# A recurrent gate's square roots taken in one step, and its scan steps spread over other places of a projection, in a two-layer decoder trunk

## The chip, the cores and the metric

One core of a Trainium2 chip (trn2) runs the whole kernel. The metric is the device time of one execution in microseconds (us). A time is told as the median of several executions; a profile is one execution of its own, with its own time.

## The reference

A two-layer decoder trunk on 256 positions of width 2048, batch 1, in float32. The change lies in layer 0, which projects the normed input to six column groups and feeds two recurrent mixers side by side:

```python
def rg_lru(xb, w_a, b_a, w_i, b_i, lam):
    r = sigmoid(einsum(xh, w_a) + b_a)
    i = sigmoid(einsum(xh, w_i) + b_i)
    log_a = -LRU_C * r * softplus(-lam)
    a = exp(log_a)
    u = sqrt(-expm1(2.0 * log_a)) * (i * xf)
    h = associative_scan(h_t = a_t * h_(t-1) + u_t)

def recurrent_mixers(h, ...):
    x_lru, y_lru, q_h, f_h, v_h, g_h = split(h @ w_in)     # six groups of 1024 columns
    lru = rg_lru(causal_depthwise_conv(x_lru), ...) * gelu(y_lru)
    hg = hgrn2(q_h, f_h, v_h, g_h, ...)                    # a gated linear recurrence, 8 heads of 128
    return concatenate([lru, hg]) @ w_out
```

A squared-ReLU MLP follows, then layer 1 (dilated attention and a second MLP) and a last norm.

## The kernel before, in words

**Matmuls.** Every weight block of 128x2048 floats (a unit) is loaded by SP into one of three `raw` buffers, then split in two: ScalarE (ACT) rounds it into `hi` with a CAST, and VectorE (DVE) makes the remainder `lo` with a TENSOR_TENSOR (`Weights.split`, L142). TensorE (PE) multiplies activations, split the same way, with both. `unit` (L249) fetches the unit two places ahead whenever one begins.

**The order of the work in layer 0.** The input projection runs in groups of 512 columns, in the order `v0 x0 x1 q0 G0 f0 q1 f1 G1 v1 g0 y0 g1 y1` (`ORDER`); `G0` and `G1` are the gate matmuls of the two halves of the LRU (`lru_gates`, L683), which share one 8x256 buffer per half (called `bufb` in the profile, gates r in its first four columns blocks, gates i in the last four). A group is four units, and a unit here is twice 12 matmuls of 128x512 (8 with `hi`, 4 with `lo`), once for each half of the positions (`tokens`, L373). So a group has eight places, one behind each run of 12 matmuls.

**The lanes.** What the mixers do beside the projection is written as Python generators, and a table (`TICKS`, L1246) says for each group which of them takes a step at which of its eight places; `.` is no step. A generator's step ends at its `yield`; when a generator is exhausted, the next one of the lane begins in the same step. The lanes that matter here:

- `e` is `lru_scan(0)`, then `lru_scan(1)` (L696). Each has four steps. The first two take two of the four feature blocks each: on DVE the product of gate i and the input (`xc`), on ACT tanh and exp of gate r, on DVE a TENSOR_SCALAR. The last two again take two blocks each: on ACT the square root, on DVE a SCALAR_TENSOR_TENSOR, a product and the scan along the positions.
- `a` and `b` are `hgrn(0)`, `hgrn(2)` and `hgrn(1)`, `hgrn(3)` (L541), two heads each; `hgrn(2)` and `hgrn(3)` are the second half, and their steps come together at one place. Step 1 turns the queries on PE (banks `pd` and `pt`) and takes their sigmoid on ACT. Step 2 turns the gates f (banks `pl`), takes three activations and two scalings of them on ACT. Step 3 makes products on DVE (`st`), rounds them on ACT and takes remainders on DVE (`bufb`, `near`). Step 4 is the first that has PE multiply them (`pd<-bufb,ones_r`, `pl<-near,ones_r`, then the same in `pt` and `pl`); steps 5 to 10 double a block size each, step 11 copies one product (`st<-pl`), step 12 multiplies with the values (`po` in the banks `pd` and `pt`) and takes squares and a copy of the result on ACT (`ho`).

**Order on the engines.** While these lanes run, ACT and DVE are held to the order in which the program issues (`InOrder`, L58). PE has an order of its own (`chain`), which runs through the matmuls of the projection and those of the lanes alike: a lane's matmul that waits holds the projection's behind it. ACT keeps the tables of one kind of function at a time (`tables`, L287): exp and tanh, sigmoid, square root; a change of kind is an ACT_TABLE_LOAD. `lut` (L291) holds functions of one kind together.

**Banks.** A group's two sums lie in two of three `p` banks. At the end of a group, ACT copies them out (`tk<-p`, L422); the first half of the next group gets the third bank, and its second half must wait for the first of these copies.

Of the kernel before, what the change touches and what calls it, by code (L numbers as in the profile page):

```python
# [15 lines left out]
AF = mybir.ActivationFunctionType  # L16
# [25 lines left out]
def trunk_kernel(ctx, tc, head, x, xtok, xback, cols, tab, masks, pos, fin, w_in, w_gate, w_out, w_qkv, w_o, w1, w2, out):  # L42
# [238 lines left out]
    def after(ins, names):  # L281
        ins = getattr(ins, "ins", ins)
        for n in names:
            tc.add_manual_dep(ins, n, NOSYNC, reason="order on one engine")
        return ins.name
# [5 lines left out]
    def lut(out_, in_, func, **kw):  # L291
        i = A.activation(out_, in_, func, **kw)
        if luts["kind"] != tables[func]:
            luts.update(kind=tables[func], before=luts["now"], now=[])
        luts["now"].append(after(i, luts["now"][:1] or luts["before"]))
# [140 lines left out]
    m = tmp.tile([P, 2], F32, name="nm2", bufs=2)  # L436
# [259 lines left out]
    def lru_scan(gp):  # L696
        gr, gi = rooms[gp][:, :4], rooms[gp][:, 4:]
        for half in range(2):
            for m in range(2 * half, 2 * half + 2):
                b = 4 * gp + m  # L700
                V.tensor_tensor(xc[:, b], xc[:, b], gi[:, m], OP.mult)
                lut(gi[:, m], gr[:, m], AF.Tanh, scale=sp4[:, b:b + 1])
                lut(gr[:, m], gr[:, m], AF.Exp, scale=sp8[:, b:b + 1])
                V.tensor_scalar(gi[:, m], gi[:, m], -1.0, 1e-30, op0=OP.mult, op1=OP.max)
            yield
        for half in range(2):
            for m in range(2 * half, 2 * half + 2):
                b = 4 * gp + m
                lut(gi[:, m], gi[:, m], AF.Sqrt)
                V.scalar_tensor_tensor(gi[:, m], gr[:, m], 1.0, gi[:, m], op0=OP.add, op1=OP.mult)  # L710
                V.tensor_tensor(xc[:, b], xc[:, b], gi[:, m], OP.mult)
                V.tensor_tensor_scan(xc[:, b], gr[:, m], xc[:, b], 0.0, op0=OP.mult, op1=OP.add)
            yield
# [19 lines left out]
    def reload():  # L733
        for j in range(2):
# [3 lines left out]
                 c=[lru_in(0, 0), lru_in(0, 1), lru_in(1, 0), lru_in(1, 1),  # L738
                    lru_gelu(0), lru_out(0, 0), lru_out(0, 1), lru_gelu(1), lru_out(1, 0), lru_out(1, 1)],
                 e=[lru_scan(0), lru_scan(1)],  # L740
                 d=[finish(0, 0), finish(0, 1), finish(1, 0), finish(1, 1)])
    InOrder.on = True
# [442 lines left out]
    with urgent():  # L1185
        for j in range(2):
            m = tmp.tile([P, 1], F32, name="fm", bufs=2)
# [175 lines left out]
```

## Time and profile before

| what | value |
| --- | --- |
| median of 3 runs (least, most) | 2119.51 us (2119.07, 2119.61) |
| the profiled execution: its own time | 2119.95 us |
| its span, first to last instruction | 2118.20 us |
| busy in the span: PE, DVE, ACT, POOL | 2105.5, 1792.0, 1321.5, 72.3 us |
| mean granted PE clock | 0.997 of full speed |
| group v1 on PE, from its first matmul to g0's | 180.03 to 207.22 us |

Rows of the timeline give the start in us from the span's beginning, the length in us, the engine, the line, the operation, output<-inputs, and how many instructions the row joins; in brackets stands how long the engine was idle ahead of it and what ended that. L68 is the line of the helper that issues nearly everything on ACT and DVE, so rows are told apart by their tiles: `hi` and `lo` are weights, `xc` and `bufb` with 256 columns the LRU, `bufb` with 512 columns and `near`, `st`, `xall` the second mixer.

### The profile page before, as it was taken

The page shows a single profiled execution, that of the slowest core. Times are in us where ns is not written, and L with a number is a line of the kernel's source. Part 1 is how long each engine was busy: PE and PEld are TensorE (multiplying, and loading weights), DVE is VectorE, ACT ScalarE, POOL GpSimd, SP SyncE. Part 2 cuts the span into 40 slices and gives each one's busy share as a digit, 9 for nine tenths or more (in the row PEclk, how much of TensorE's full clock was granted, in tenths as well). Part 3 has the DMA queues.
Part 4 walks back from the last instruction along what each step waited for, and adds up shares of the span by engine and source line. Part 5 has one row for each costly group of instructions (what it writes and reads, how often), then busy time and mean ns, then how long its engine had stood idle before and what let it go on. Part 6 is the DMA issues. An engine that isn't in the chain of part 4 may idle for free.

```text
span 2118.2 us, 24850 instructions
## 1 busy us (share of the span) xinstructions
PE 2105.5 (99%) x9712; PEld 1752.8 (83%) x9712; DVE 1792.0 (85%) x1742; ACT 1321.5 (62%) x1356; POOL 72.3 (3%) x89
## 2 busy tenths in 40 slices
PE   9999999999999999999999999999999999999998
PEld 7888788888888888888888888888888888888887
DVE  7686878988888888889998888798988987988887
ACT  7576556675566566566665666576755755755764
POOL 0000000000000000000000000000000000000000
PEclk9999999999999999999999999999999999999999
DMA  8544456787787878877778667477778778787884
GB/s 344 181 162 159 157 208 209 248 267 236 244 262 252 258 230 274 253 242 237 263 252 255 203 214 238 179 236 236 243 244 272 242 237 276 245 250 239 277 261 157
DMA packets 70453, 500.15 MB, mean 236 GB/s; under 512 B 7872, under 2 KB 8128, under 8 KB 10560
## 3 DMA queue, kind: packets, MB, share of 16 engines
q1 hardware_dynamic: 58176, 413.29, 50.7%
q0 software_dynamic: 11872, 84.94, 22.1%
q8 instruction: 76, 1.25, 0.2%
q10 hardware_dynamic: 288, 0.34, 0.0%
q14 instruction: 41, 0.34, 0.0%
HBM read 496.44 MB, written 2.10 MB: 235 GB/s over the span
## 4 chain that ended last, share of the span: by engine, by line
PE 98%; ACT 1%; DVE 1%; DMA 0%; SPq 0%; issue 0%; DVEq 0%
PE p L261 62%; PE pd L261 15%; PE po L261 14%; PE pt L261 3%; PE pl L264 2%; PE pl L261 1%; DMA both_in<-in_head 0%; ACT xall L68 0%; ACT L68 0%; ACT hi L68 0%; PE po L264 0%; ACT ho L68 0%; DVE xall L68 0%; DVE xc L68 0%; DVE bufb L68 0%; ACT bufb L68 0%
## 5 line engine op out<-in xcount | busy, mean ns | idle before, releaser
L68 ACT CAST hi<-raw 128x2048 fp32r<-128x2048 f32 (+1 forms) x364 | 660.1, 1819 | 518.5 <-PE p L261 300.7
L68 DVE TENSOR_TENSOR lo<-raw,hi 128x2048 fp32r<-128x2048 f32 (+1 forms) x364 | 788.9, 2172 | 137.2 <-ACT hi L68 136.6
L261 PE MATMUL p<-hi,bufa 128*128 128x512 f32 x2000 | 504.2, 393 | 0.7 <-ACT hi L68 0.6
L261 PEld LDWEIGHTS p<-hi,bufa 128*128 128x128 f32 x2000 | 373.2, 189 | 76.8 <-ACT hi L68 1.3
L261 PE MATMUL p<-hi,bufb 128*128 128x512 f32 x1264 | 318.3, 391 | 0.0
L68 DVE TENSOR_TENSOR lo<-s,hi 128x2048 fp32r<-128x2048 f32 x120 | 274.3, 2286 | 12.9 <-ACT hi L68 10.9
L261 PEld LDWEIGHTS p<-hi,bufb 128*128 128x128 f32 x1264 | 236.3, 188 | 48.5 <-DVE bufb L68 0.2
L261 PE MATMUL p<-lo,bufa 128*128 128x512 f32 x1000 | 270.2, 390 | 0.0
L68 ACT CAST hi<-s 128x2048 fp32r<-128x2048 f32 x120 | 229.4, 1911 | 58.2 <-PE pd L261 23.6
L261 PEld LDWEIGHTS p<-lo,bufa 128*128 128x128 f32 x1000 | 188.1, 188 | 40.0 <-DVE lo L68 0.7
L261 PE MATMUL p<-lo,bufb 128*128 128x512 f32 x632 | 173.0, 390 | 0.0
L261 PEld LDWEIGHTS p<-lo,bufb 128*128 128x128 f32 x632 | 118.7, 188 | 24.7
L68 DVE TENSOR_TENSOR lo<-t,hi 128x2048 fp32r<-128x2048 f32 x40 | 91.5, 2287 | 4.4 <-ACT hi L68 4.0
L68 ACT CAST hi<-t 128x2048 fp32r<-128x2048 f32 x40 | 76.6, 1915 | 28.2 <-PE pd L261 12.3
L68 DVE TENSOR_TENSOR s<-s,raw 128x2048 f32<-128x2048 f32 x40 | 91.3, 2284 | 1.1 <-DMA raw<-in_w_qkv 1.1
L68 DVE TENSOR_TENSOR s<-raw,t 128x2048 f32<-128x2048 f32 x40 | 91.4, 2286 | 0.3 <-DMA raw<-in_w_o 0.2
L68 ACT ACTIVATE y<-y 128x512 f32<-128x512 f32 x112 | 70.5, 629 | 31.8 <-DVE y L68 31.0
L261 PE MATMUL pd<-hi,bufa 128*128 128x512 f32 x352 | 88.2, 393 | 0.0
L261 PE MATMUL p<-hi,formx 128*128 128x512 f32 x352 | 87.7, 391 | 0.0
L68 DVE SCALAR_TENSOR_TENSOR xall<-p,nm,xall 128x512 f32<-128x512 f32 x64 | 47.9, 748 | 43.3 <-PE p L261 43.3
L261 PE MATMUL po<-hi,bufb 128*128 128x512 f32 (+1 forms) x320 | 78.2, 386 | 0.0
L261 PEld LDWEIGHTS p<-hi,formx 128*128 128x128 f32 x352 | 65.7, 188 | 13.4
(309 smaller groups left out, 2573.1 us busy)
## 6 DMA issues: line engine op xcount, KB each, us to landing
raw<-in_w SPq DMA_DIRECT2D x224, 1024.0 KB, 6.9
raw<-in_w_in SPq DMA_DIRECT2D x45, 1024.0 KB, 4.8
raw<-in_w_qkv SPq DMA_DIRECT2D x42, 1024.0 KB, 7.2
t<-in_w SPq DMA_DIRECT2D x32, 1024.0 KB, 7.2
t<-in_w POOLq DMA_DIRECT2D x32, 1024.0 KB, 9.0
s<-in_w POOLq DMA_DIRECT2D x32, 1024.0 KB, 9.2
raw<-in_w_out SPq DMA_DIRECT2D x15, 1024.0 KB, 4.8
raw<-in_w_o SPq DMA_DIRECT2D x15, 1024.0 KB, 4.8
```

The lines of the kernel that those rows point to most:

```text
L68: i = call(*args, **kw)
L261: chain[:] = [after(T.matmul(*args, **kw), chain)]
L264: chain[:] = [after(T.transpose(out_, in_, ident), chain)]
```

## The change

```diff
@@ lru_scan
             yield
+        for m in range(4):
+            lut(gi[:, m], gi[:, m], AF.Sqrt)
         for half in range(2):
             for m in range(2 * half, 2 * half + 2):
                 b = 4 * gp + m
-                lut(gi[:, m], gi[:, m], AF.Sqrt)
                 V.scalar_tensor_tensor(gi[:, m], gr[:, m], 1.0, gi[:, m], op0=OP.add, op1=OP.mult)
@@ TICKS
-    "v1": "ab . ab e ab e ab e",
-    "g0": "ab e ab . ab . ab .",
+    "v1": "ab e ab e ab e ab e",
+    "g0": "ab . ab . ab . ab .",
```

Two things. In both halves of the LRU, the third step now takes all four square roots, and the fourth takes none. And `lru_scan(1)` has its four steps at the places 1, 3, 5 and 7 of v1 (counted from 0), where it had them at 3, 5 and 7 of v1 and 1 of g0. The first half keeps its places in f0. PE's order of instructions is the same in both kernels.

**ACT, at the place 1 of v1** (`sp4` and `sp8` are the scales of tanh and exp, `st<-pl` is step 11 of the second mixer's first half, `c__91` the gate biases; the difference of the two kernels):

```order
 L68 ACTIVATE bufb_1497<-pl,c__91 128x256 x2
-L68 CAST hi<-raw 128x2048 x2
+L68 CAST hi<-raw 128x2048
+L68 ACTIVATE bufb_1497<-bufb_1497,sp_364 128x256
+L68 ACT_TABLE_LOAD
+L68 ACTIVATE bufb_1497<-bufb_1497,sp_362 128x256
+L68 ACTIVATE bufb_1497<-bufb_1497,sp_364 128x256
+L68 ACTIVATE bufb_1497<-bufb_1497,sp_362 128x256
+L68 CAST hi<-raw 128x2048
 L68 COPY st<-pl 128x2x128 x2
```

The first scan step, with its table load, now stands ahead of the CAST of v1's last unit and of the two copies of step 11, and not behind them.

**ACT, from the place 6 of v1 on, before** (`pd` and `pt` hold the queries of step 1, `tk<-p` are the copies at the end of v1; behind the last row follow step 2's activations, one more load and the roots of the other two blocks):

```order
L68 COPY ho_1688<-pt_1681 128x512
L68 ACTIVATE bufb3_1497<-bufb3_1497,sp4_364 128x256
L68 ACTIVATE bufb3_1497<-bufb3_1497,sp8_362 128x256
L68 ACTIVATE bufb3_1497<-bufb3_1497,sp4_364 128x256
L68 ACTIVATE bufb3_1497<-bufb3_1497,sp8_362 128x256
L68 CAST hi_1717<-raw_1715 128x2048
L68 ACT_TABLE_LOAD
L68 ACTIVATE xall_79<-pd_1732 128x2x2x128
L68 ACTIVATE xall_79<-pt_1740 128x2x2x128
L68 ACT_TABLE_LOAD
L68 ACTIVATE bufb3_1497<-bufb3_1497 128x256 x2
L68 ACTIVATE tk_1769<-p_1558,nr2_317 128x512
```

and now:

```order
L68 COPY ho_1696<-pt_1689 128x512
L68 ACT_TABLE_LOAD
L68 ACTIVATE bufb3_1497<-bufb3_1497 128x256 x4
L68 CAST hi_1727<-raw_1725 128x2048
L68 ACT_TABLE_LOAD
L68 ACTIVATE xall_79<-pd_1742 128x2x2x128
L68 ACTIVATE xall_79<-pt_1750 128x2x2x128
L68 ACTIVATE tk_1777<-p_1558,nr2_317 128x512
L68 ACTIVATE tk_1777<-p_1559,nr2_317 128x512
L68 CAST hi_1784<-raw_1782 128x2048
```

The four roots stand together behind step 12's copies and ahead of a unit's CAST; the sigmoid of step 1, step 2 and, later, the output gate's sigmoid share one table load. From v1's beginning to that sigmoid there were six table loads and are three.

**DVE, ahead of step 3** (`st<-xall` is step 3's first product, before):

```order
L68 TENSOR_TENSOR lo_1777<-raw_1774,hi_1776 128x2048
L68 SCALAR_TENSOR_TENSOR bufb3_1497<-bufb3_1497 128x256
L68 TENSOR_TENSOR xc_403<-xc_403,bufb3_1497 128x256
L68 SCALAR_TENSOR_TENSOR xc_403<-bufb3_1497,xc_403 128x256
L68 SCALAR_TENSOR_TENSOR bufb3_1497<-bufb3_1497 128x256
L68 TENSOR_TENSOR xc_403<-xc_403,bufb3_1497 128x256
L68 SCALAR_TENSOR_TENSOR xc_403<-bufb3_1497,xc_403 128x256
L68 TENSOR_TENSOR st_1851<-xall_79 128x2x256
```

and now:

```order
L68 SCALAR_TENSOR_TENSOR bufb3_1497<-bufb3_1497 128x256
L68 TENSOR_TENSOR xc_403<-xc_403,bufb3_1497 128x256
L68 SCALAR_TENSOR_TENSOR xc_403<-bufb3_1497,xc_403 128x256
L68 SCALAR_TENSOR_TENSOR bufb3_1497<-bufb3_1497 128x256
L68 TENSOR_TENSOR xc_403<-xc_403,bufb3_1497 128x256
L68 SCALAR_TENSOR_TENSOR xc_403<-bufb3_1497,xc_403 128x256
L68 TENSOR_TENSOR lo_1785<-raw_1782,hi_1784 128x2048
L68 TENSOR_TENSOR st_1851<-xall_79 128x2x256
```

The last two scans (the SCALAR_TENSOR_TENSOR that writes `xc`) changed places with the remainder of a unit of g0, and their roots are no longer taken just ahead of them.

## The prediction

> **What bounds the kernel now.** I read the page's first part, then PE's waits, then PE's timeline around each wait.
>
> ```profile
> PE 2105.5 (99%) x9712; PEld 1752.8 (83%) x9712; DVE 1792.0 (85%) x1742; ACT 1321.5 (62%) x1356; POOL 72.3 (3%) x89
> PE pd L261 <- ACT bufb L68: 1.5, 1, 1.5
> PE pt L261 <- ACT bufb L68: 0.9, 1, 0.9
> PE pd L261 <- DVE bufb L68: 0.6, 1, 0.6
> PE pt L261 <- DVE bufb L68: 0.3, 1, 0.3
> ```
>
> PE bounds the kernel: it is busy for 2105.5 us of a span of 2118.2. So an edit on ACT and DVE is worth only what it takes from PE's waits, and four of the few waits there are (3.3 us together) stand at one place, where step 4 of the second half's `hgrn` waits for step 3's products. The timeline of PE at this place, in g0:
>
> ```profile
> 220.81 1.07 PE L261 MATMUL p<-lo,bufa 128*128 128x512 f32 x4
> ...
> 223.35 0.50 PE L261 MATMUL pd<-bufb,ones_r 128*128 128x512 f32 x1 [1.48 <-ACT bufb L68]
> ...
> 227.21 0.79 PE L261 MATMUL pt<-bufb,ones_r 128*128 128x512 f32 x1 [0.34 <-DVE bufb L68]
> ...
> 228.23 3.62 PE L261 MATMUL p<-hi,bufa 128*128 128x512 f32 x8
> ...
> 235.74 1.07 PE L261 MATMUL pl<-xall,kc 128*128 128x128 f32 x8
> ```
>
> and at the same step of the first half, in q1, where nothing waits:
>
> ```profile
> 137.48 1.07 PE L261 MATMUL p<-lo,bufa 128*128 128x512 f32 x4
> 138.39 0.61 PE L261 MATMUL pd<-bufb,ones_r 128*128 128x512 f32 x2
> ...
> 139.77 1.99 PE L261 MATMUL p<-hi,bufa 128*128 128x512 f32 x8
> ...
> 145.22 1.07 PE L261 MATMUL pl<-xall,kc 128*128 128x128 f32 x8
> ```
>
> The instructions are the same. Undisturbed, step 4 begins 0.91 us after the `lo` row, takes 1.38 (138.39 to 139.77), and step 5 follows 5.45 later (145.22). In g0, step 4 could begin at 220.81 + 0.91 = 221.72, and step 5 at 221.72 + 6.83 = 228.55. It begins at 235.74. So the place costs **7.19 us**, more than twice the idle time that is listed: the rest is the clock.
>
> ```profile
> 222.30:225.70 3.40, 1.24 (x4) 0.67 (x4) 3.30 (x7) 1.32 (x3) 0.00 (x0) 1.00 0.00 0
> 225.80:232.50 6.70, 6.08 (x15) 4.51 (x15) 6.67 (x12) 2.95 (x5) 0.00 (x0) 0.50 0.26 83
> ```
>
> (The stretch, its length, then the busy time of PE and of the others.) The granted clock, third figure from the end, is 0.50 from 225.8 to 232.5, 6.7 us long, behind 3.4 us in which PE was busy for 1.24. That is why eight matmuls at 228.23 take 3.62 us, and eight at 139.77 take 1.99.
>
> What holds step 3 up is DVE:
>
> ```profile
> 210.10 0.42 DVE L68 SCALAR_TENSOR_TENSOR bufb<-bufb 128x256 f32<-128x256 f32 x1
> ...
> 213.13 2.27 DVE L68 TENSOR_TENSOR lo<-raw,hi 128x2048 fp32r<-128x2048 f32 x1
> 218.95 0.42 DVE L68 SCALAR_TENSOR_TENSOR bufb<-bufb 128x256 f32<-128x256 f32 x1 [3.56 <-ACT bufb L68]
> ...
> 221.98 0.67 DVE L68 TENSOR_TENSOR st<-xall 128x512 f32<-128x512 f32 x1
> ...
> 227.08 0.42 DVE L68 TENSOR_TENSOR near<-st,near 128x256 fp32r<-128x256 f32 x1
> 218.50 0.72 ACT L68 ACTIVATE bufb<-bufb 128x256 f32<-128x256 f32 x2
> ```
>
> DVE waits 3.56 us for the second pair of roots (ACT, 218.50), scans two blocks in 3.03 us (218.95 to 221.98), and only then begins step 3, which ends at 227.50 with `near`; PE takes up the projection at 228.23, 0.7 us behind.
>
> **The change part by part.** In the new order DVE still does two scans ahead of step 3, but waits for no root there. When it gets there is a chain through ACT and DVE from v1 on; it starts at a row that the change leaves where it is:
>
> ```profile
> 185.57 4.49 DVE L68 TENSOR_TENSOR lo<-raw,hi 128x2048 fp32r<-128x2048 f32 x2
> 189.98 0.42 DVE L68 TENSOR_TENSOR xc<-xc,bufb 128x256 f32<-128x256 f32 x1
> 207.91 2.28 DVE L68 TENSOR_TENSOR lo<-raw,hi 128x2048 fp32r<-128x2048 f32 x1
> 190.49 0.51 ACT L68 ACTIVATE bufb<-bufb,sp 128x256 f32<-128x256 f32 x1
> ...
> 193.68 1.89 ACT L68 CAST hi<-raw 128x2048 fp32r<-128x2048 f32 x1
> 197.01 0.28 ACT L68 ACTIVATE ho<-pd 128x128 f32<-128x128 f32 x1 [1.44 <-PE pd L261]
> ...
> 200.32 1.05 ACT L68 ACTIVATE bufb<-bufb,sp 128x256 f32<-128x256 f32 x2
> ...
> 202.49 1.90 ACT L68 CAST hi<-raw 128x2048 fp32r<-128x2048 f32 x1
> 204.41 1.28 ACT L68 ACT_TABLE_LOAD   x1
> 205.70 0.60 ACT L68 ACTIVATE xall<-pd 128x512 f32<-128x512 f32 x1
> ...
> 208.73 1.25 ACT L68 ACTIVATE tk<-p,nr 128x512 f32<-128x512 f32 x2
> 206.33 0.88 DVE L68 SCALAR_TENSOR_TENSOR xall<-pd,omlb,xall 128x256 f32<-128x256 f32 x2 [3.96 <-ACT xall L68]
> ```
>
> 1. One remainder, not two, stands ahead of the first `xc` product. A remainder takes 2.19 us from start to start (207.91 to the scan row 210.10), so the product starts at 185.57 + 2.19 = 187.76, and the first scan step ends with ACT's CAST at 193.68 - 2.22 = 191.46, done at 193.35.
> 2. That CAST's remainder takes DVE from 193.4 to 195.6; then comes the second step's product, and 0.51 later (189.98 to 190.49) its tanh, at 196.1. The two pairs take 2.17 (200.32 to 202.49), so the CAST of g0's first unit runs from 198.3 to 200.2.
> 3. Step 12's squares and copies take 3.31 (197.01 to 200.32): to 203.5. Then the new load, 1.28, to about 204.9; four roots for 1.4 (two took 0.72); a CAST of 1.9, to 208.1; the load of the sigmoid, to 209.4; the sigmoid of 0.60, to 210.0.
> 4. DVE has scanned the first two blocks by then (3.03 from 205.3). Its four products of step 1 take 1.58 (206.33 to 207.91): 211.6. A remainder, 2.19: 213.8. The two other scans, 3.03: 216.8. A remainder, 2.19: **219.0**, where step 3 begins, instead of 221.98.
>
> So step 3 and all that follows on DVE shifts by **3.0 us**. Its input is there: step 2's activations end on ACT at about 217, as before, since the copies ahead of them come some 1.6 us later and a load and a pair of roots less stand between. Step 3 ends at 227.50 - 3.0 = 224.5, and PE takes up the projection at about 224.6. Nominally it would be 221.72 + 1.38 = 223.1, so some 1.5 us of the wait remain. With the clock whole, step 5 follows 5.45 us later, at 230.1, against 235.74: **5.6 us are saved**. Of these, 3.6 are in the restart (228.23 to 224.6) and 2.1 in matmuls that are no longer slow (7.51 from restart to step 5 before, 5.45 now).
>
> The rest, each costed at nothing or nearly:
> - Three table loads of 1.28 us less on ACT. ACT is busy 62% of the span, and only those on the chain above count.
> - The second half of g0's first unit waits for the first `tk<-p`. It follows item 3's sigmoid and its twin (0.5 each), so it runs from 210.4 to about 211.1. PE wants the bank here:
>
> ```profile
> 210.74 2.07 PE L261 MATMUL p<-hi,bufa 128*128 128x512 f32 x8
> 195.47 1.50 PE L261 MATMUL pd<-tk,st 128*128 128x128 f32 x12
> raw<-in_w_in SPq DMA_DIRECT2D x45, 1024.0 KB, 4.8
> ```
>
>   That is a new wait of 0.3 us, but it ends ahead of step 4, where PE waits for DVE in any case; so it adds nothing to the sum.
> - Step 11's copies now stand behind the moved CAST, at 193.3 to 194.1; PE wants them at 195.47. Cover 1.4 us; beyond that each us costs one.
> - SP's queue: the buffer of v1's last unit comes free at 195.6 and not at 190.06, and the next load into it lands 4.8 us later, 200.4. Its CAST stands at 211.4 in the new order. POOL has no work here.
> - The first half's roots: one CAST moves back by two roots, 0.6 us. Its remainder starts behind a scan in both kernels:
>
> ```profile
> 116.46 1.90 ACT L68 CAST hi<-raw 128x2048 fp32r<-128x2048 f32 x1
> 119.78 2.27 DVE L68 TENSOR_TENSOR lo<-raw,hi 128x2048 fp32r<-128x2048 f32 x1
> ```
>
>   The CAST would end at 119.0, ahead of 119.78, so nothing moves.
> - After step 5, PE is the bound again, and ACT and DVE run earlier too, DVE by only 3.0 us at first. So up to 0.2 us may be lost at step 5, where the copies `kc` come close; I count none.
>
> The profiled execution took 2119.95 us, 0.44 above the median, so the sum goes on the median: 2119.51 - 5.6 = **2113.9 us**.
>
> Two rules were weighed. ACT's row of a table load is 1.28 us, its neighbours lie 0.02 us from it (202.49 + 1.90 to 204.41, and to 205.70), and the chain above holds three loads. The Trainium skill, page "ScalarE: Activation LUTs", section "What ACT_TABLE_LOAD costs", gives about 1.28 us and a drain of 1.38 us on top for every change. By that, as an estimate from that page, step 3 would begin some 4 us later and the gain would be 1.5 us; the trace here has no room for such a drain, so it gets no chance of its own. In the other rule the skill speaks for the change: in the page "TensorE: Matmul & The Clock Gate", section "What's actually happening", the clock falls only after about 3.4 us of idleness. By this rule it would stay whole in the new kernel; but here it fell with no wait over 1.48 us, so the trace does not bear that limit out.
>
> **The rivals.**
> *The clock falls all the same.* The remaining 1.5 us of waiting lies in some 3 us of step 4. If that is enough, the half clock lasts about as long as before, 6.7 us, and costs up to 3.4 us: gain 2.2, **2117.3 us**. For it: the clock fell with matmuls between the waits. Against it: there PE was busy for 1.24 of 3.4 us; here, with 1.5 us of waits in such a stretch, it would be for 1.9, somewhat over half. And early in the trace half a microsecond of idleness leaves the clock whole:
>
> ```profile
> 5.00:6.00 1.00, 0.50 (x2) 0.37 (x3) 0.96 (x3) 0.60 (x2) 0.00 (x0) 1.00 1.01 372
> ```
>
> *The wait goes entirely*, because the chain runs 1.5 us earlier than I add up: gain 7.2, **2112.3 us**.
> *Slower: the bank.* The `tk` copy stands behind four roots and two loads, and holds PE at 210.74. I have it 0.3 us late. If ACT's chain runs late by x, this wait and step 3 both come late by x, and PE loses it whole. The gain is gone from x = 5.6 on, and with a second fall of the clock (3.4 us) from x = 2.2 on; an x of 6.5 with it gives 2119.5 + 4.3 = **2123.8 us**. Against it: each term is a measured row, and between 194.1 and 196.1 ACT is idle.
> *The change does nothing that shows*: another instruction at DVE's head holds step 3 as long as now, **2119.5 us**. The order shows none.
>
> **How the numbers follow.** The forecast has 0.64, the wait that goes entirely 0.05, the falling clock 0.18, nothing 0.06, slower 0.07. About 0.2%, 4.2 us, is what a measurement of this kernel can tell from no change. The forecast's 5.6 lies 1.4 above that, and its chain may be off by about 1, so I put 0.04 of it below: faster 0.65, same 0.28, slower 0.07. The range goes from the whole wait gone (2112.2) to the falling clock (2117.6), which holds 0.85.
>
> **What the new profile would show.** Right: `st<-xall` on DVE near 219.0, PE back in the projection near 224.6, `pl<-xall,kc` near 230.1, the clock at 1.00 from 224 to 234, two waits of PE left at step 4 (near 0.4 and 0.9 us) and one of 0.3 ahead of 210.74's row. Wrong: a clock of 0.50 anywhere in g0; a wait at 195.47; or a time after 250 that isn't shifted by the same 5.6 us, which would mean that loads or DVE take the gain back later.

## The result, and the profile after

The changed kernel takes 2114.26 us (median of 12 executions, 2113.83 to 2114.61), the kernel before beside it 2119.34 us (12 executions, 2118.21 to 2120.23): ratio 0.9976, with a 95% interval from 0.9967 to 0.9985. The profiled execution took 2114.33 us and spans 2112.6, against 2119.95 and 2118.2.

The busy times of the page and the waits of PE, of the changed kernel:

```profile
PE 2103.1 (100%) x9712; PEld 1751.9 (83%) x9712; DVE 1791.8 (85%) x1742; ACT 1317.2 (62%) x1353; POOL 72.3 (3%) x89
PE pt L261 <- DVE bufb L68: 0.6, 1, 0.6
PE pt L261 <- ACT bufb L68: 0.2, 1, 0.2
```

Of the four waits at step 4, two of 0.6 and 0.2 us are left. PE's busy time fell by 2.4 us though it has the same 9712 instructions. Most of that is the clock: from PE's return to the projection to step 5 it took 7.51 us before and takes 5.47 now (224.50 to 229.97). The timeline of PE in g0:

```profile
208.84 1.07 PE L261 MATMUL p<-lo,bufa 128*128 128x512 f32 x4
...
210.71 2.12 PE L261 MATMUL p<-hi,bufa 128*128 128x512 f32 x8
...
221.73 0.62 PE L261 MATMUL pd<-bufb,ones_r 128*128 128x512 f32 x2
...
222.79 0.51 PE L261 MATMUL pt<-bufb,ones_r 128*128 128x512 f32 x1 [0.21 <-ACT bufb L68]
223.93 0.50 PE L261 MATMUL pt<-bufb,ones_r 128*128 128x512 f32 x1 [0.63 <-DVE bufb L68]
...
224.50 2.00 PE L261 MATMUL p<-hi,bufa 128*128 128x512 f32 x8
...
229.97 1.23 PE L261 MATMUL pl<-xall,kc 128*128 128x128 f32 x8
```

and the windows of the same stretches as before (length, busy time of PE, PEld, DVE, ACT, POOL, then the granted clock):

```profile
222.30:225.70 3.40, 2.55 (x13) 1.77 (x12) 3.37 (x5) 2.66 (x3) 0.00 (x0) 1.00 0.15 60
225.80:232.50 6.70, 6.70 (x35) 5.62 (x34) 6.70 (x12) 2.84 (x5) 0.00 (x0) 1.00 0.46 159
```

Step 4 takes 2.77 us (221.73 to 224.50) where 1.38 is undisturbed, so 1.4 us of its wait remain. The clock stays at 1.00, no wait stands ahead of step 12's matmuls (the forecast had named one there as a sign of being wrong), and the whole span is 5.6 us shorter, so nothing later takes the gain back. For all runs below I use one distance, **the place**: from the first `lo` row of g0 to step 5's first `pl<-xall,kc`. It doesn't depend on where a whole profile begins; the rows of PE ahead of 180 us differ by up to 0.7 us between two profiles. In the kernel before the first `lo` row is this:

```profile
209.03 1.07 PE L261 MATMUL p<-lo,bufa 128*128 128x512 f32 x4
```

So the place was 235.74 - 209.03 = 26.71 us before. It is 229.97 - 208.84 = 21.13 now, 5.58 less, and undisturbed it would be 19.52 (12.69 from 209.03 to 221.72, and the 6.83 of the prediction).

### The profile page after: what moved, and what is told of

Same layout as the page of the kernel before. It is cut to its first block, busy times and chain, and to the rows that moved or that the text cites. A ratio compares the mean times of both kernels' runs of the same rounds, so it can differ in the third digit from the quotient of the medians.

```text
span 2112.6 us, 24846 instructions
## 1 busy us (share of the span) xinstructions
PE 2103.1 (100%) x9712; PEld 1751.9 (83%) x9712; DVE 1791.8 (85%) x1742; ACT 1317.2 (62%) x1353; POOL 72.3 (3%) x89
## 4 chain that ended last, share of the span: by engine, by line
PE 98%; DVE 1%; ACT 1%; issue 0%; DVEq 0%; ACTq 0%
PE p L261 62%; PE pd L261 15%; PE po L261 14%; PE pt L261 3%; PE pl L264 2%; PE pl L261 1%; DVE lo L68 0%; ACT hi L68 0%; DVE xall L68 0%; PE po L326 0%; ACT L68 0%; ACT bufb L68 0%; PE po L264 0%; ACT ho L68 0%; DVE st L68 0%
```

## The experiments

Eleven runs, on three chips; the kernel before ran on each of these chips too (2119.34, 2119.26 and 2118.96 us). Differences below are to the kernel before on the same chip.

### The grouped roots alone

The new generator with the old table.

```diff
-    "v1": "ab e ab e ab e ab e",
-    "g0": "ab . ab . ab . ab .",
+    "v1": "ab . ab e ab e ab e",
+    "g0": "ab e ab . ab . ab .",
```

> The four roots in one step, the steps at the places of before. Theory (the time follows the moment at which DVE begins step 3, and the clock): with the roots of all four blocks taken at the place 7 of v1, DVE's last two scans in g0 no longer wait 3.56 us for ACT. On DVE the remainder at 213.1 ends at 215.3, the scans take 3.0, step 3 starts near 218.4 instead of 222.0, PE is back in the projection near 224.0 instead of 228.2, the clock stays whole: 6.1 us less than before, about 1 us less than the whole change, so the moved places are worth nothing or a little less than nothing. Rival A (the places do it: a free place 1 in g0): same as before. Rival B (each table load less is worth the same, three loads for 5.1 us; here two are gone): 3.4 us less.

Measured: 2113.92 us (8 executions), ratio 0.9975 [0.9965, 0.9985], 5.4 us less than before. On PE and on DVE:

```profile
208.38 1.07 PE L261 MATMUL p<-lo,bufa 128*128 128x512 f32 x4
...
229.03 1.23 PE L261 MATMUL pl<-xall,kc 128*128 128x128 f32 x8
```

```profile
212.48 2.27 DVE L68 TENSOR_TENSOR lo<-raw,hi 128x2048 fp32r<-128x2048 f32 x1
214.66 0.42 DVE L68 SCALAR_TENSOR_TENSOR bufb<-bufb 128x256 f32<-128x256 f32 x1
...
217.69 0.67 DVE L68 TENSOR_TENSOR st<-xall 128x512 f32<-128x512 f32 x1
```

The 3.56 us for which DVE waited for a root are gone (214.66 follows its remainder at once), though the last scan step still stands in g0. The place is 20.65, 6.06 less than before and 0.48 less than in the whole change: step 3 begins 9.31 us behind the first `lo` row, in the whole change 9.77. So the roots edit alone does all that the change does. The expected 6.1 us is what the place shows; the medians show 5.4, and the lead over the whole change at the place is half of the expected 1 us.

### The places alone

The old generator with the new table (the two lines above with their signs exchanged, in the kernel before).

> The steps at the new places, each step with its own two roots, as before. Theory: ACT has the load and the second pair of roots ahead of the copy that frees the bank, and another load ahead of step 2, so step 2 ends near 219.8 and a CAST stands between it and step 3's rounding; the copy comes 1.4 us late for PE, step 3's last row ends near 226.1 on DVE, PE is back near 226.2 instead of 228.2: 1.8 us less than before if the clock falls again, 3.9 us less if it does not. Rival A (the places do it): 5 us less. Rival B (one load is gone): 1.7 us less, with step 3 at any time.

Measured: 2116.14 us (11 executions), 0.9985 [0.9976, 0.9994], 3.2 us less. PE's timeline and two windows:

```profile
208.54 1.07 PE L261 MATMUL p<-lo,bufa 128*128 128x512 f32 x4
...
211.83 2.11 PE L261 MATMUL p<-hi,bufa 128*128 128x512 f32 x8 [1.34 <-ACT tk L68]
...
231.44 1.23 PE L261 MATMUL pl<-xall,kc 128*128 128x128 f32 x8
```

```profile
209.41:212.83 3.42, 2.08 (x13) 1.65 (x12) 3.42 (x5) 3.41 (x6) 0.00 (x0) 1.00 0.00 0
...
223.07:226.48 3.41, 2.22 (x11) 1.51 (x10) 3.34 (x6) 2.32 (x3) 0.00 (x0) 1.00 0.00 0
```

The place is 22.90, 3.81 less, at full clock. With both pairs of roots, and a table load for each, ahead of the copy that frees the bank, PE waits 1.34 us for that copy: the bank wait of the prediction is real, and the grouped roots shrink it to 0.16 in the whole change. The gains of the two edits (6.06 and 3.81) don't add: each takes away the same wait.

### The waits kept, the clock held up

The kernel before, with 12 matmuls whose sums nobody reads, in the idle times of step 4 in the second half.

```diff
+ if c2 > 1 and to is pd:
+     spin = psc.tile([P, 512], F32, name="po", bufs=1)
+     for _ in range(((6, 2), (3, 1))[c2 - 2][n]):
+         mm(spin, ones_r, bufa[:, 0], start=True, stop=True)
  mm(to, ones_r, part, start=not n, stop=n == 1)
```

> The kernel before, with twelve matmuls of 128x512 more in step 4 of the second half: six ahead of the first matmul in pd, two behind it, three ahead of the first in pt, one behind it; they read ready operands, and nobody reads their result. Theory (2.1 us of the 7.2 are the fallen clock): the fillers lie in PE's waits (1.48, 0.63, 0.85 and 0.34 us), the clock stays at 1.00, PE comes back to the projection near 227.6 and step 5 begins near 233.0 instead of 235.7: 2.7 us less than before. Rival (the matmuls behind the wait are slow for another reason, such as the loads or the other engines at work beside them): they stay slow, and the time is that of before or up to 1 us more.

Measured: 2117.80 us (11 executions), 0.9992 [0.9983, 1.0001]: 1.5 us less, with no change just inside the interval. PE:

```profile
208.31 1.07 PE L261 MATMUL p<-lo,bufa 128*128 128x512 f32 x4
...
227.08 2.00 PE L261 MATMUL p<-hi,bufa 128*128 128x512 f32 x8
...
232.56 1.23 PE L261 MATMUL pl<-xall,kc 128*128 128x128 f32 x8
```

By the profile it is clear: the projection resumes 18.77 us behind the first `lo` row, hardly earlier than before (228.23 - 209.03 = 19.20), and then runs at full clock, so step 5 follows in 5.48 us where it took 7.51. The place is 24.25, 2.46 less. By the time it is not settled: the medians show 0.9 less than the profile, whose execution (2117.03 us) is the fastest of the eleven.

### The first half's roots alone

```diff
-        for m in range(4):
+        for m in range(0 if gp else 4):
             lut(gi[:, m], gi[:, m], AF.Sqrt)
...
+                if gp:
+                    lut(gi[:, m], gi[:, m], AF.Sqrt)
```

with the old table.

> The four roots in one step for the first half only (group f0); the second half as before. Theory: nothing on PE's path moves, the same as before within what can be told, and step 4 of the second half with the same waits. Rival (part of the gain comes from the first half): 0.5 us or more less, with PE's rows ahead of 180 us earlier than in the kernel before by as much.

Measured: 2119.13 us (10 executions), 1.0000 [0.9990, 1.0009]. The four waits at step 4 are those of before, and the place is 26.43, 0.28 less with nothing changed there:

```profile
208.31 1.07 PE L261 MATMUL p<-lo,bufa 128*128 128x512 f32 x4
...
234.74 1.07 PE L261 MATMUL pl<-xall,kc 128*128 128x128 f32 x8
```

The clock explains it. Its records in the trace have the fall at 224.36 us here and at 225.77 in the kernel before, in both for 6.83 us; counted from the first `lo` row that is 16.05 and 16.74 us. The window up to the fall, and the next:

```profile
220.95:224.36 3.41, 1.29 (x5) 0.67 (x4) 3.34 (x7) 1.02 (x2) 0.00 (x0) 1.00 0.00 0
224.36:227.78 3.42, 2.22 (x7) 1.48 (x6) 3.35 (x6) 2.53 (x3) 0.00 (x0) 0.50 0.02 5
```

The same spell began 0.7 us earlier against the work, so that more of it lay in idle time (PE was busy for 2.22 us of its first 3.4). So the prediction's "nothing moves" holds for the first half.

### Two more loads ahead of the roots

The changed kernel with two one-column activations that nobody reads, which make ACT load two more tables in the second half.

```diff
+        if gp:
+            lut(spare, epsc, AF.Sigmoid)
+            lut(spare, epsc, AF.Exp)
         for m in range(4):
             lut(gi[:, m], gi[:, m], AF.Sqrt)
```

> The changed kernel with two more table loads on ACT ahead of the four roots of the second half (a sigmoid and an exp of one column each, whose results nobody reads). Theory (a load costs its row, 1.28 us, and ACT's chain carries it on): the copy that frees the bank comes about 3.0 us later, so PE waits some 3 us in g0's first unit, and step 3 begins near 221.6 instead of 218.6. Without a fall of the clock step 5 begins near 233.0, 3.0 us more than the changed kernel; with a fall after the wait in g0's first unit, near 235.0, 5.0 us more, and then step 4 waits for nothing. Rival (the drain that the Trainium skill, page ScalarE: Activation LUTs, section What ACT_TABLE_LOAD costs, gives on top of each load; its figure, 1.38 us, is an estimate for here): the copy comes 5.7 us later, and the time is 5.8 us or more above the changed kernel. Rival (ACT's chain has slack that I don't see): less than 1 us more.

Measured: 2117.37 us (11 executions), 0.9991 [0.9982, 1.0000], 1.9 us less than before. ACT, then PE and its windows:

```profile
203.59 1.28 ACT L68 ACT_TABLE_LOAD   x1
...
205.10 1.28 ACT L68 ACT_TABLE_LOAD   x1
...
206.60 1.28 ACT L68 ACT_TABLE_LOAD   x1
207.90 1.34 ACT L68 ACTIVATE bufb<-bufb 128x256 f32<-128x256 f32 x4
```

```profile
209.18 1.07 PE L261 MATMUL p<-lo,bufa 128*128 128x512 f32 x4
...
214.06 3.30 PE L261 MATMUL p<-hi,bufa 128*128 128x512 f32 x8 [2.94 <-ACT tk L68]
...
233.52 0.73 PE L261 MATMUL pl<-xall,kc 128*128 128x128 f32 x5
```

```profile
211.24:214.65 3.41, 0.59 (x3) 0.50 (x4) 1.90 (x6) 3.40 (x6) 0.00 (x0) 1.00 0.00 0
214.65:218.06 3.41, 3.41 (x10) 2.64 (x9) 3.34 (x4) 3.41 (x6) 0.00 (x0) 0.50 0.16 22
```

Each load with its small activation costs 1.5 us (203.59, 205.10, 206.60). PE waits 2.94 us for the bank, the clock falls behind it, and step 4 then waits for nothing. The place is 24.34: 3.21 more than in the changed kernel, of which 3.0 are the bank (209.18 to 214.06, against 208.84 to 210.71), 1.6 the clock, and -1.4 the wait of step 4 that the delay covers. The clock did fall, but for 3.41 us, half as long as before, so the result lies between what was expected with a fall and without one.

### The last scan step moved behind step 3

Two tables with the changed generator: the step in g0 but behind step 3, and in y0, the next group.

```diff
-    "v1": "ab e ab e ab e ab e",
-    "g0": "ab . ab . ab . ab .",
+    "v1": "ab e ab e ab e ab .",
+    "g0": "ab . ab e ab . ab .",
```

> The changed kernel with the last scan step at the place 3 of g0, behind step 3 and ahead of step 4's work on DVE. Theory: step 4's wait goes as with the scans in y0 (PE back near 223.4), but step 4's products on DVE come 2.0 us later, so step 5 waits for its copies kc until 230.1 and 232.3: 1.8 us more than the changed kernel, two waits of PE at step 5 in place of those at step 4. Rival (step 5 has the room): 1.1 us less than the changed kernel.

Measured: 2117.44 us (11 executions, 2115.86 to 2118.01), 0.9990 [0.9981, 0.9999]. Four lie at 2115.86 to 2116.22, seven at 2117.39 to 2118.01. The profile is of one of the four; PE and two windows:

```profile
223.12 2.00 PE L261 MATMUL p<-hi,bufa 128*128 128x512 f32 x8
...
230.02 0.69 PE L261 MATMUL pl<-xall,kc 128*128 128x128 f32 x4 [1.27 <-DVE st L68]
232.10 0.70 PE L261 MATMUL pl<-xall,kc 128*128 128x128 f32 x4 [1.39 <-DVE st L68]
```

```profile
227.34:230.75 3.41, 2.11 (x11) 1.36 (x9) 3.39 (x8) 0.52 (x2) 0.00 (x0) 1.00 0.53 223
230.75:234.17 3.42, 2.07 (x11) 1.85 (x12) 3.42 (x5) 2.32 (x3) 0.00 (x0) 1.00 0.02 5
```

Step 4 no longer waits, but the two scans now stand ahead of DVE's products for step 5, and PE waits there, for 2.7 us. The wait has moved by one step of the mixer. The lower four are near what was expected (1.6 us more than the changed kernel, where 1.8 was forecast); the seven above were not. (The two windows are used at the end.)

```diff
-    "v1": "ab e ab e ab e ab e",
+    "v1": "ab e ab e ab e ab .",
...
-    "y0": "ab d ab d ab . ab d",
+    "y0": "ab d ab d ab e ab d",
```

> The changed kernel with the last scan step (two blocks, 3.0 us of DVE) at the place 5 of y0 instead of 7 of v1. Theory: step 3 begins near 215.6 on DVE, but its first rounding on ACT stands behind a CAST that ends near 218.8, so its first remainder starts near 219.4 instead of 220.5; PE is back near 223.4, 1.1 us sooner than in the changed kernel, and in y0 DVE has room: 1.1 us less than the changed kernel, 6.7 less than before from the row ahead of g0's step 2 to step 5. Rival A (DVE's scans are all that holds step 3): PE is back at 223.1, with no wait at all, 1.4 us less. Rival B (the gain is given back in y0, where the scans delay a step on DVE): the same as the changed kernel, with a new wait of PE after 255.

Measured: 2113.18 us (8 executions), 0.9972 [0.9962, 0.9982], 6.1 us less. No wait is left in g0:

```profile
208.76 1.07 PE L261 MATMUL p<-lo,bufa 128*128 128x512 f32 x4
...
223.39 2.00 PE L261 MATMUL p<-hi,bufa 128*128 128x512 f32 x8
...
228.86 1.22 PE L261 MATMUL pl<-xall,kc 128*128 128x128 f32 x8
```

The place is 20.10: 1.03 less than in the changed kernel and 0.6 above the undisturbed 19.52.

### Three kernels again, and why one has two heaps

The changed kernel, the roots alone and the step in y0 ran once more, unedited, on one chip.

> The changed kernel as it is, beside the next two on the same chip. Theory: 2114.3 us, 5 us less than before.

> The four roots in one step, the places of before, once more beside the changed kernel. Theory: PE's rows from g0's step 2 to step 5 are 0.5 us shorter than in the changed kernel, so 0.3 to 0.5 us less than it. Rival (the places are worth something after all): more than the changed kernel.

> The changed kernel with its last scan step in y0, once more beside the changed kernel. Theory: 1.0 to 1.1 us less than the changed kernel on the same chip. Rival (the difference of the first time lay in the chip): within 0.3 us of it.

Measured: 2114.35 (0.9979 [0.9970, 0.9987]), 2113.63 (0.9974 [0.9964, 0.9984]) and 2113.18 us (0.9972 [0.9961, 0.9983]), of 11, 9 and 7 executions. The places are 21.13, 20.69 and 20.09, each within 0.04 of its first value. On this chip the roots alone are 0.7 us faster than the whole change (0.3 to 0.5 were expected; the places differ by 0.44), and the step in y0 1.2 us.

The last kernel fills the waits of the step behind step 3 with matmuls that nobody reads:

```diff
+ if c2 > 1 and c == 2:
+     spin = psc.tile([P, 512], F32, name="po", bufs=1)
+     for _ in range(5):
+         mm(spin, ones_r, bufa[:, 0], start=True, stop=True)
```

> The kernel with the last scan step behind step 3, with ten matmuls of 128x512 more in step 5: five ahead of the first product with kc, five ahead of the second, reading ready operands, their result read by nobody. That kernel's times lay in two heaps, 2115.9 to 2116.2 and 2117.4 to 2118.0. Theory (in some executions its two waits at step 5 let the clock fall, in others not): with the waits filled the clock never falls, and all times lie in the lower heap, near 2116. Rival (the heaps come from the loads or from DVE): two heaps as before, or one at the upper level.

Measured: 2116.28 us (11 executions), 0.9987 [0.9978, 0.9996]. Nine lie at or below 2116.45, two between the heaps at 2116.86 and 2117.16; the upper heap is gone. Step 5's second half comes no earlier than without the filler (here 232.26 - 222.82 = 9.44 us from the projection's restart to the next `hi` row, there 232.54 - 223.12 = 9.42):

```profile
222.82 2.00 PE L261 MATMUL p<-hi,bufa 128*128 128x512 f32 x8
...
231.81 0.70 PE L261 MATMUL pl<-xall,kc 128*128 128x128 f32 x4 [0.24 <-DVE st L68]
232.26 2.09 PE L261 MATMUL p<-hi,bufa 128*128 128x512 f32 x8
```

So what made seven of eleven executions some 1.9 us longer (the medians of the two heaps, 2117.80 and 2115.90) was taken away by busy time that does no work. A fall of the clock behind the idle step 5 fits, and the mean granted clock on record for each execution bears it out: without the filler it is 0.999 in the four of the lower heap, and in the upper heap 0.998 in five and 0.999 in two; with the filler it is 0.999 in all eleven. The kernel with two more loads, whose profile has 3.41 us of half clock, has 0.998 in six executions and 0.999 in five. Where in an execution of the upper heap the clock fell is not shown, since none was profiled.

## Why the prediction was right, point by point

**What bounds the kernel: right.** The cost of the place was put at 7.19 us, of which the waits are listed and the rest is the clock. The run that filled the waits and so held the clock up gave 2.46 us of it back (at the place; its median, 1.5 us less, is not clear of no change); the run without any wait in g0 gave 6.62 (26.71 - 20.09).

**The chain: right, each term measured 0.1 to 0.4 us earlier than forecast.** ACT and DVE of the changed kernel, at the rows that the chain goes through:

```profile
191.27 1.89 ACT L68 CAST hi<-raw 128x2048 fp32r<-128x2048 f32 x1
...
203.25 1.28 ACT L68 ACT_TABLE_LOAD   x1
204.54 1.34 ACT L68 ACTIVATE bufb<-bufb 128x256 f32<-128x256 f32 x4
```

```profile
213.40 0.42 DVE L68 SCALAR_TENSOR_TENSOR bufb<-bufb 128x256 f32<-128x256 f32 x1
...
218.61 0.68 DVE L68 TENSOR_TENSOR st<-xall 128x512 f32<-128x512 f32 x1
```

| step of the chain | forecast | measured |
| --- | --- | --- |
| the CAST behind the first scan step (term 1) | 191.46 | 191.27 |
| the load ahead of the roots (term 3) | 203.5 | 203.25 |
| the four roots | 204.9 | 204.54 |
| DVE's first scans in g0 (term 4) | 213.8 | 213.40 |
| `st<-xall`, where step 3 begins | 219.0 | 218.61 |
| PE back in the projection | 224.6 | 224.50 |
| step 5 on PE | 230.1 | 229.97 |

The first 0.2 us are the profile's own (the `lo` row at 208.84 and not 209.03). Measured from that row, step 3 begins 9.77 us behind it, where 219.0 - 209.03 = 9.97 was reckoned, and step 5 21.13 where 21.07 was.

**The small terms.** The bank wait of 0.3 us came out at 0.16 (210.71, where the old distance of 1.71 gives 208.84 + 1.71 = 210.55). The "up to 0.2" at step 5 is 0.16: its row takes 1.23 us and not 1.07. Of the two waits left at step 4, near 0.4 and 0.9 by the forecast, 0.2 and 0.6 are listed. Measured from row to row they are 0.4 and 1.0, and so the 1.4 us of the sum: from the start of the matmuls ahead (222.18) to the first in `pt` 0.61 us, and from there to the last two (224.26) 1.47, where the kernel with two more loads, which waits for nothing there, has 0.23 and 0.47.

**The sum: right at the place, 0.5 us too large in the median.** 5.6 us was forecast; the place measures 5.58 and the two profiled executions 5.62. The medians differ by 5.1. I put the sum on the median although before's profiled execution lay above it (2119.95 against 2119.34 here). The executions of before spread over 2.0 us, those of the changed kernel over 0.8. Where the spell of half clock begins changes the loss, as the first half's run shows with its 0.28 us. The executions of before also differ in how much slow clock they have: of the 81 that ran beside the experiments, 57 have a mean granted clock of 0.997, as the profiled one has, and a median of 2119.53 us; 24 have 0.998 or 0.999 and a median of 2118.64. So the 2.1 us for the clock are the price of the common execution, which is the one that was profiled. With the 0.997 executions alone, before's median would lie 0.2 to 0.3 us higher on each of the three chips; the rest of the 0.5 us is not explained.

**What the prediction didn't see.** It priced the two edits as one. The runs show that the roots edit alone takes 6.06 us off the place and the moved places, beside it, put 0.48 back: DVE reaches step 3 half a microsecond later. The reason lies in step 1's sigmoid on ACT, for which DVE's products wait. In the changed kernel and with the roots alone it is

```profile
208.99 0.60 ACT L68 ACTIVATE xall<-pd 128x512 f32<-128x512 f32 x1
205.05 0.60 ACT L68 ACTIVATE xall<-pd 128x512 f32<-128x512 f32 x1
```

Against the first `lo` row that is 0.15 us behind (208.84) and 3.33 ahead (208.38). The moved places put the load and the four roots ahead of it (2.54 us, 203.25 to 205.79), and in the new order it comes 3.48 us later in all. In exchange one pair of scans, 3.03 us, stands ahead of DVE's products and not behind them. From these products to step 3 DVE doesn't pause in either kernel, so 3.48 - 3.03 = 0.45 us are lost; measured are 0.46 (9.77 and 9.31).

**The rivals.** *The falling clock* did not come: PE was busy for 2.55 of 3.4 us at step 4, more than the 1.9 that I reckoned, and the mean clock is 0.999 in all 23 executions of the changed kernel. *The wait that goes entirely* is what the step in y0 gives (2113.18, against 2112.3 forecast for it), not the change. *The bank* is a real mechanism with a wrong price: with the copy 3.0 us later, the formula with a second fall says 5.6 - 3.0 - 3.4, a loss of 0.8; measured is a gain of 1.9. The fall lasted 3.4 us and cost 1.6, and the 1.4 us of step 4's wait vanished under the delay. With these numbers, the change would lose only from a copy some 5.4 us late (5.6 - 1.6 + 1.4).

The price of a table load decided between 5.6 and 1.5 us, and the row of 1.28 us with the next instruction 0.02 us behind it held: two more loads, each with its activation, moved the roots' load by 1.5 us apiece. The Trainium skill, page "ScalarE: Activation LUTs", section "What ACT_TABLE_LOAD costs", adds a drain of about 1.38 us to every switch; these three switches have no room for it.

## What to carry to other kernels

Where an engine in order waits for a chain through two others, find which instruction of that chain waits first, and ask what else could stand there: here two scans that nobody needed yet held up the products that the busiest engine waited for. Price the wait by the distance between two rows of that engine against the same distance where nothing waits, since the slow clock behind the idle time cost 2.1 of the 7.2 us and stands in no list of waits. Then move the step once more: one place behind its rival it made a new wait of 2.7 us, one group later none.

## What the runs showed of the hardware

**The gate of the clock counts in windows of 3.413 us that run freely, and it is the busy share of one window that decides.** The records of the granted clock have its rise at the start of each kernel and its falls. In the kernel before the fall comes 221.867 us behind the rise, which is 65.00 times 3.4133; with the first half's roots alone it comes at 64.00, with two more loads at 61.00, and the spells of half clock (6.827, 6.827 and 3.413 us) are two, two and one of the same. So the windows can be laid on the trace from the rise on. They run freely: the rise comes between 3.9 and 7.1 us behind the beginning of the span in the thirteen profiles. The kernel before, the window that ends at the fall and the next:

```profile
222.36:225.77 3.41, 1.24 (x4) 0.67 (x4) 3.31 (x7) 1.39 (x3) 0.00 (x0) 1.00 0.00 0
225.77:229.18 3.41, 2.76 (x7) 1.97 (x8) 3.38 (x5) 2.46 (x3) 0.00 (x0) 0.50 0.02 5
```

The clock fell behind windows with 1.24, 1.29 and 0.59 busy us, and stayed whole behind the emptiest windows of other kernels laid in the same way: 2.07 and 2.11 (the step behind step 3), 2.08 and 2.22 (the places alone). The limit lies between 1.29 and 2.07 of 3.41. At the end of the kernel, where PE runs out of work, the clock falls in all thirteen profiles, and that narrows it: the fullest window behind which it fell held 1.35 us (the changed kernel once more), the emptiest behind which it stayed whole 1.92 (the step behind step 3). The Trainium skill, page "TensorE: Matmul & The Clock Gate", section "What's actually happening", has the same free-running window of 3413 ns; it has the clock fall after an idle window, and here a window that was 38% busy (1.29 of 3.41) was enough.

**One window that PE nearly fills lets it rise again.** With two more loads PE was busy for all of the first slow window, and the clock rose after 3.41 us. In the kernel before it was busy for 2.76 of it, with the first half's roots alone for 2.22, and a second slow window followed: 6.83 us. It need not be all of the window: at its start, the kernel before has its rise at 3.90 us, behind a window with 2.85 busy us. So this limit lies between 2.76 and 2.85. The length of the spell is why the falling clock was priced too high in the rivals: a wait that is over when the clock falls costs half as much of it as one that goes on.

**The phase decides near the limit.** With the step behind step 3, the profiled execution had its idle time split between two windows of 2.11 and 2.07; a window of the same length placed otherwise would have held far less:

```profile
228.75:232.16 3.41, 0.76 (x6) 0.62 (x5) 3.41 (x10) 1.27 (x5) 0.00 (x0) 1.00 0.10 43
```

With 0.76 the clock would have fallen, by the limit above. The phase differs from one execution to the next (against the first `lo` row by 0.7 us between the two profiles of the changed kernel and by 1.5 us between those of the step in y0), so this would make two heaps of times out of one program, as were measured. The mean clocks of the heaps agree, and so do the two kinds of executions of the kernel before; it is the likeliest cause, and still not seen in a profile of the upper heap.
